# Eight storage orders for the split weights, and pairs for four chunks of x, in a two-layer fp32 decoder trunk

## The chip, the cores and the metric

One core of one Trainium2 chip runs the whole program in one launch. The metric is device microseconds of that core, the median of three runs.

## The reference

Two layers; each normalises x (512 tokens, 2048 features), makes one wide projection, runs two attention groups of eight heads on it, gates them, projects back and adds. Everything is fp32.

```python
for l in range(DEPTH):                       # 2
    h = _rms_norm(x, norm_g[l])
    proj = jnp.einsum('bsd,de->bse', h, w_in[l])
    q_a, k_a, v_a, z_a, c_q, c_kv, k_r, z_b = jnp.split(proj, split_points, axis=-1)
    ...
    o_a = _diff_attention(qa, ka, va, lam, rel_bias_table)     # 8 heads, two softmax maps each
    ...
    q_b = jnp.einsum('bsr,re->bse', _rms_norm(c_q, mla_q_norm_g[l]), w_uq[l])
    kv = jnp.einsum('bsr,re->bse', _rms_norm(c_kv, mla_kv_norm_g[l]), w_ukv[l])
    ...
    o_b = _mla_attention(q_nope, q_rope, k_nope, k_rope, v_b)  # 8 heads
    ...
    mixed = jnp.concatenate([o_a, o_b], axis=-1)
    x = x + jnp.einsum('bse,ed->bsd', mixed, w_out[l])
return _rms_norm(x, final_norm_g)
```

## The kernel before

x is kept feature-major: sixteen chunks of 128 features by 512 tokens. An fp32 product is made of three passes in the rounded type fp32r: each operand is split into a high part (the rounded copy) and a low part (what rounding left), and `mm3` adds high by high, high by low and low by high into one PSUM bank. A matmul has a stationary operand, 128 by 128, which a weight load (PEld in the profile) brings into the array, and a moving operand, mostly 128 by 512, which streams past it. In `mm3` the weight part is stationary and the x part moves. In `job_v` it is the other way round.

The weights come as 290 blocks of 128 by 1024, in the order in which TensorE uses them. `WStream` fetches block i into a buffer `raw` (two of them, two blocks ahead), and one block ahead of its use splits it: ScalarE casts `raw` into `whi` (L94), VectorE subtracts into `wlo` (L95). Each of `whi` and `wlo` has two buffers, so the split of the next block waits until TensorE is done with the one before the current one. A full block of `mm3` work is 8 chunks by 3 passes, 24 matmuls.

A block has a kind. "std" is the usual one; "kr" is one block per layer with its own layout; a callable kind puts a few blocks into a slot of another tile. The blocks of `b_kouter` (the first projection of layer 0, chunk by chunk as x arrives, and the diff group's V) and of `b_uv` (the MLA group's V) are "std" too.

`split_into` splits the chunks of x into tiles `x0` to `x15`, one tile per chunk, which holds the high part in its first 512 words and the low part in the next 512. The same tiles `x0` to `x7` are reused at the end of a layer for the gated outputs of the MLA heads, which are the first half of the operands of the output projection (`job_out_half`).

The order of the work on TensorE and of the DMA issues on SyncE and GpSimd is written out by hand (`run_jobs` walks the jobs and slips attention steps between them). The order on ScalarE and VectorE is left to the framework's scheduler.

Of the kernel before, what the change touches and what calls it, by code (L numbers as in the profile page):

```python
# [9 lines left out]
F32 = mybir.dt.float32  # L10
F32R = mybir.dt.float32r
AF = mybir.ActivationFunctionType
ALU = mybir.AluOpType
AX = mybir.AxisListType

P = 128
T = 512
# [44 lines left out]
class WStream:  # L62
# [3 lines left out]
    def __init__(self, nc, pool, src, dma_ahead=2, split_ahead=1):  # L66
        self.nc, self.pool, self.src = nc, pool, src
        self.descs, self.raw, self.parts = [], {}, {}
        self.nd = self.ns = self.i = 0
        self.da, self.sa = dma_ahead, split_ahead  # L70
# [7 lines left out]
    def _split(self, i):  # L78
        nc = self.nc
        _, width, kind = self.descs[i]  # L80
        r = self.raw.pop(i)
        if callable(kind):
            a, b = kind()
        else:
            a = self.pool.tile([P, 1024], F32R, tag="whi", name=f"whi{i}", bufs=2)
            b = self.pool.tile([P, 1024], F32R, tag="wlo", name=f"wlo{i}", bufs=2)
        if kind == "kr":
            for t, k0 in ((a, 0), (b, 8)):
                tv = t.rearrange("p (k s c) -> p k s c", s=2, c=64)
                rv = r.rearrange("p (k c) -> p k c", c=64)[:, k0:k0 + 8, :]  # L90
                nc.scalar.copy(out=tv[:, :, 0, :], in_=rv)
                nc.vector.tensor_tensor(out=tv[:, :, 1, :], in0=rv, in1=tv[:, :, 0, :].bitcast(F32), op=ALU.subtract)
        else:
            nc.scalar.copy(out=a[:, :width], in_=r[:, :width])  # L94
            nc.vector.tensor_tensor(out=b[:, :width], in0=r[:, :width], in1=a[:, :width].bitcast(F32), op=ALU.subtract)  # L95
        self.parts[i] = (a, b)
# [12 lines left out]
    def get(self, ahead=True):  # L109
        i = self.i  # L110
        self.i += 1
        if ahead:
            self.ahead()
        return self.parts.pop(i)


def fold(w):

    return w.reshape(-1, P, w.shape[1]).transpose(1, 0, 2).reshape(P, -1)
# [25 lines left out]
def trunk(ctx, tc, blocks, xf, gains, diff_lambda, rel_bias_table, onehot, tables, wb, outf):  # L145
    nc = tc.nc
# [8 lines left out]
    def t_(shape, dt, tag, bufs):  # L155
        uid[0] += 1
        return sb.tile(shape, dt, tag=tag, name=f"{tag}_{uid[0]}", bufs=bufs)
# [8 lines left out]
    def f32(ap):  # L166
        return ap.bitcast(F32)
# [6 lines left out]
        return (lambda a: fold(a[w[0]][w[1]][r0:r0 + 1024, c0:c0 + P])), 1024, kind  # L174

    def b_kouter(w, c0, j):
        return (lambda a: fold(a[w[0]][w[1]][j * 256:(j + 1) * 256, c0:c0 + T])), 1024, "std"

    def b_kr(w):
        return (lambda a: fold(a[w[0]][w[1]][:, C_KR:C_KR + 64])), 1024, "kr"  # L180
# [15 lines left out]
    def b_uv(l, q, j):  # L196

        def block(a):
            w = a["w_ukv"][l][j * 256:(j + 1) * 256, q * 1024:(q + 1) * 1024]
            return fold(w.reshape(256, 4, 256)[:, :, P:].reshape(256, T))  # L200
        return block, 1024, "std"


    ident = sb.tile([P, P], F32, name="ident")
# [51 lines left out]
    def split_into(k, src, scale):  # L256

        both = t_([P, 2, T], F32R, f"x{k}", 1)
        hi, lo = both[:, 0, :], both[:, 1, :]
        if scale is None:  # L260
            nc.scalar.copy(out=hi, in_=src)
            nc.vector.tensor_tensor(out=lo, in0=src, in1=f32(hi), op=ALU.subtract)
        else:
            nc.scalar.activation(out=hi, in_=src, func=AF.Copy, scale=scale)
            nc.vector.scalar_tensor_tensor(out=lo, in0=src, scalar=scale, in1=f32(hi), op0=ALU.mult, op1=ALU.subtract)
        return hi, lo

    def load_x(k):
        if k % 2 == 0 and XA + k < KC:
            fetch_x(XA + k, 2, nc.sync)  # L270
        xh[k], xl[k] = split_into(k, xt[k], g_norm(0, k))
        square_into(xt[k], k, KC - 1)
# [68 lines left out]
    def job_kouter(src2d, c0, accs, xload):  # L341
        ws.descs += [b_kouter(src2d, c0, j) for j in range(8)]

        def gen():
            accs.extend([p_("s", 2), p_("s", 2), p_("o", 1), p_("acc", 3)])
            ws.ahead()
            xload(0)
            for j in range(8):
                hi, lo = ws.get()
                if j == 0:  # L350
                    xload(1)
                for kk in range(2):
                    kc = 2 * j + kk
                    if kc + 2 < KC:
                        xload(kc + 2)
                    for i in range(4):
                        c = slice(kk * T + i * P, kk * T + (i + 1) * P)
                        mm3(accs[i], hi[:, c], lo[:, c], xh[kc], xl[kc], kc == 0, kc == KC - 1)
                    yield
        return 16, gen  # L360
# [511 lines left out]
    xnew, pairs = {}, {}  # L872
    for l in range(DEPTH):
# [33 lines left out]
        def v_mla(q, l=l, ckvn=ckvn):  # L907
            return job_v([b_uv(l, q, j) for j in range(2)], lambda kc: (ckvn[kc][:, 0, :], ckvn[kc][:, 1, :]), None)

        def v_diff(q, wi=wi):  # L910
            return job_v([b_kouter(wi, C_V + q * T, j) for j in range(8)], lambda kc: (xh[kc], xl[kc]), True)
# [13 lines left out]
        def split_mix(i, mix=mix, ms=mslot):  # L925
            def f():
                ms[i] = split_into(i, mix[8 + i], None)
            return f

        def out_evac(d, l=l):  # L930
            def f(acc):
                r = st["res"].pop(d)
                xn = t_([P, T], F32, "ma", 8) if d < 8 else tmp()
                nc.vector.tensor_tensor(out=xn, in0=acc, in1=r, op=ALU.add)
                nc.gpsimd.dma_start(out=xres[l + 1][d], in_=xn)
                square_into(xn, d, KC - 1)
                if d >= 8:
                    xh[d], xl[d] = split_into(d, xn, g_norm(l + 1, d))
                xnew[d] = xn
            return f  # L940
# [151 lines left out]
```

## Time and profile before

| | |
|---|---|
| median of 3 runs | 1840.79 us (1840.78 to 1840.84) |
| the profiled execution | 1841.41 us, its span 1839.6 us |
| TensorE matmul (PE) busy | 1795.7 us, 98% |
| weight loads (PEld) busy | 1488.3 us, beside the matmuls |
| VectorE (DVE) busy | 1021.9 us, 56% |
| ScalarE (ACT) busy | 878.8 us, 48% |
| TensorE clock granted, mean | 0.99 of full |

A matmul's listed duration is longer than the distance to the next one, because matmuls are pipelined. What one of them costs is read from the starts of two that follow each other; the text calls this distance the pitch.

### The profile page before, as it was taken

What the parts mean: (1) busy time and instruction counts of PE and PEld (TensorE: products, weight loads), DVE (VectorE), ACT (ScalarE), POOL (GpSimd) and SP (SyncE); (2) the same over time, 40 slices, a digit from 0 to 9 for tenths busy, and PEclk for the clock granted to TensorE, in tenths of its full rate; (3) what the DMA queues carried; (4) which work ended last, traced back from release to release, by engine and by line L of the source; (5) the groups of instructions that cost most, each with busy time, mean ns of one, the idle gap of its engine ahead of it and who ended that gap; (6) DMA issues with size and microseconds to landing.
All of it is one profiled execution on the core that took longest, in us unless ns stands there. A gap on an engine that the chain in (4) does not pass through costs nothing.

```text
span 1839.6 us, 21822 instructions
## 1 busy us (share of the span) xinstructions
PE 1795.7 (98%) x8348; PEld 1488.3 (81%) x8348; DVE 1021.9 (56%) x1903; ACT 878.8 (48%) x1548; POOL 38.0 (2%) x74
## 2 busy tenths in 40 slices
PE   9958999999999999999999999999999999999997
PEld 7837888888888888888888888888888888888886
DVE  6616556553777366743355565465366654784334
ACT  6406555542666355622344466465355544663332
POOL 0000000000000000010000000000000000000000
PEclk9978999999999999999999999999999999999999
DMA  5352222223222332344432322222332323233333
GB/s 212 95 85 80 73 71 89 83 86 96 93 83 78 103 92 86 97 138 147 145 121 92 96 75 65 75 91 85 95 91 87 94 90 92 77 92 119 119 116 131
DMA packets 55621, 181.11 MB, mean 98 GB/s; under 512 B 6908, under 2 KB 11004, under 8 KB 55517
## 3 DMA queue, kind: packets, MB, share of 16 engines
q1 hardware_dynamic: 48828, 159.00, 27.7%
q0 software_dynamic: 6400, 20.19, 4.5%
q8 instruction: 66, 1.08, 0.2%
q10 hardware_dynamic: 288, 0.52, 0.1%
q14 instruction: 39, 0.31, 0.1%
HBM read 168.68 MB, written 11.01 MB: 98 GB/s over the span
## 4 chain that ended last, share of the span: by engine, by line
PE 94%; DMA 3%; DVE 2%; ACT 1%; issue 0%; DVEq 0%; ACTq 0%; SPq 0%
PE pacc L319 23%; PE pacc L321 23%; PE pacc L320 23%; PE pacc L428 3%; PE pacc L430 3%; PE pacc L429 3%; DMA raw<-in_blocks_dram 3%; PE ptp L672 2%; PE po L689 1%; PE po L690 1%; PE po L688 1%; PE po L428 1%; PE ps L320 1%; PE po L430 1%; PE po L429 1%; PE ps L321 1%
## 5 line engine op out<-in xcount | busy, mean ns | idle before, releaser
L94 ACT CAST whi<-raw 128x1024 fp32r<-128x1024 f32 (+1 forms) x282 | 292.2, 1037 | 634.9 <-PE pacc L320 428.1
L319 PE MATMUL pacc<-x,whi 128*128 128x512 f32 (+1 forms) x1472 | 583.1, 396 | 11.5 <-ACT whi L94 11.5
L321 PE MATMUL pacc<-x,wlo 128*128 128x512 f32 (+1 forms) x1472 | 575.1, 391 | 0.0
L320 PE MATMUL pacc<-x,whi 128*128 128x512 f32 (+1 forms) x1472 | 574.4, 390 | 0.0
L95 DVE TENSOR_TENSOR wlo<-raw,whi 128x1024 fp32r<-128x1024 f32 (+1 forms) x282 | 340.8, 1208 | 340.9 <-ACT whi L94 332.3
L319 PEld LDWEIGHTS pacc<-x,whi 128*128 128x128 f32 x1472 | 278.2, 189 | 63.7 <-ACT whi L94 12.0
L321 PEld LDWEIGHTS pacc<-x,wlo 128*128 128x128 f32 x1472 | 277.2, 188 | 60.0 <-DVE wlo L95 0.8
L320 PEld LDWEIGHTS pacc<-x,whi 128*128 128x128 f32 x1472 | 277.8, 189 | 50.9
L319 PE MATMUL pacc<-mb,whi 128*128 128x512 f32 (+1 forms) x400 | 158.5, 396 | 0.0
L321 PE MATMUL pacc<-mb,wlo 128*128 128x512 f32 (+1 forms) x400 | 156.4, 391 | 0.7 <-DVE wlo L95 0.7
L320 PE MATMUL pacc<-mb,whi 128*128 128x512 f32 (+1 forms) x400 | 156.3, 391 | 0.0
L665 ACT ACTIVATE sa<-sa,m 128x128 f32<-128x128 f32 (+3 forms) x128 | 71.9, 561 | 119.2 <-DVE m L663 118.2
L663 DVE CUSTOM_DVE_ANT_0 sa<-ps,cs 128x128 f32<-128x128 f32 (+3 forms) x128 | 62.2, 486 | 83.3 <-PE ptp L672 30.7
L539 DVE TENSOR_TENSOR tmp<-pacc,rstd 128x512 f32<-128x512 f32 x64 | 44.1, 689 | 94.9 <-PE pacc L321 94.9
L321 PEld LDWEIGHTS pacc<-mb,wlo 128*128 128x128 f32 x400 | 75.2, 188 | 19.1 <-DVE wlo L95 1.5
L320 PEld LDWEIGHTS pacc<-mb,whi 128*128 128x128 f32 x400 | 75.3, 188 | 16.3
L319 PEld LDWEIGHTS pacc<-mb,whi 128*128 128x128 f32 x400 | 75.3, 188 | 16.1
L678 ACT CAST pth<-ptp 128x128 fp32r<-128x128 f32 (+3 forms) x128 | 53.7, 420 | 46.8 <-PE ptp L672 46.5
L428 PE MATMUL pacc<-whi,x 128*128 128x512 f32 x192 | 75.9, 395 | 0.0
L430 PE MATMUL pacc<-whi,x 128*128 128x512 f32 x192 | 74.8, 390 | 0.0
L429 PE MATMUL pacc<-wlo,x 128*128 128x512 f32 x192 | 74.8, 390 | 0.0
L679 DVE TENSOR_TENSOR ptl<-ptp,pth 128x128 fp32r<-128x128 f32 (+3 forms) x128 | 61.7, 485 | 4.2 <-ACT pth L678 2.4
(247 smaller groups left out, 2347.6 us busy)
## 6 DMA issues: line engine op xcount, KB each, us to landing
raw<-in_blocks_dram SPq DMA_DIRECT2D x282, 512.0 KB, 3.5
cs<-brow POOLq DMA_DIRECT2D x16, 256.0 KB, 3.0
cs<-in_x_dram POOLq DMA_DIRECT2D x16, 256.0 KB, 4.2
cs<-xres POOLq DMA_DIRECT2D x16, 256.0 KB, 2.9
out_dram<-x SPq DMA_DIRECT2D x16, 256.0 KB, 2.2
mb<-in_x_dram SPq DMA_DIRECT2D x7, 512.0 KB, 6.5
brow<-pth POOLq DMA_DIRECT2D x1, 2560.0 KB, 56.6
raw<-in_blocks_dram SPq DMA_DIRECT2D x8, 256.0 KB, 2.6
```

The costliest lines, as they stand in the source:

```text
L94: nc.scalar.copy(out=a[:, :width], in_=r[:, :width])
L95: nc.vector.tensor_tensor(out=b[:, :width], in0=r[:, :width], in1=a[:, :width].bitcast(F32), op=ALU.subtract)
L319: nc.tensor.matmul(acc, wh, rh, start=first, stop=False)
L320: nc.tensor.matmul(acc, wh, rl, start=False, stop=False)
L321: nc.tensor.matmul(acc, wl, rh, start=False, stop=last)
L428: nc.tensor.matmul(accs[t], xhi[:, c], hi[:, w], start=kc == 0, stop=False)
L429: nc.tensor.matmul(accs[t], xhi[:, c], lo[:, w], start=False, stop=False)
L430: nc.tensor.matmul(accs[t], xlo[:, c], hi[:, w], start=False, stop=kc == n - 1)
L663: nc.vector.tensor_tensor_reduce(out=s[:, :n], in0=ps[:, :n], in1=bias, scale=-scale, scalar=3.0e38, op0=ALU.add, op1=ALU.min, accum_out=m ...
L665: nc.scalar.activation(out=s[:, :n], in_=s[:, :n], func=AF.Exp, scale=-1.0, bias=m[:, 0:1], accum_out=m[:, 1:2])
L678: nc.scalar.copy(out=view(h["ph"]), in_=pv)
L679: nc.vector.tensor_tensor(out=view(h["pl"]), in0=pv, in1=f32(view(h["ph"])), op=ALU.subtract)
```

## The change

A std block gets one tile `w` of 2048 + 48 words in place of `whi` and `wlo`. Where the words of the high and the low part lie in it goes by the block's number modulo eight: "apart" is the order of before (each part is one run of 1024 words); in "pairs" the high and the low word of one weight lie side by side, so that a part is read and written in steps of 2 words (8 bytes), at four different starts (0, 16, 32 and 48 words into the tile); in "groups" the eight chunks lie innermost, so that one chunk's 128 words lie 8 words (32 bytes) apart; in "both" they lie 16 words (64 bytes) apart; the eighth is "apart" 16 words further on. The blocks of `b_kouter` and `b_uv` become "plain": two runs of 1024 as before, in the common tile. Four chunks of x, 4 to 7, have their two parts in pairs (steps of 8 bytes), in the input projections as in the output projection.

```diff
-            a = self.pool.tile([P, 1024], F32R, tag="whi", name=f"whi{i}", bufs=2)
-            b = self.pool.tile([P, 1024], F32R, tag="wlo", name=f"wlo{i}", bufs=2)
+            t = self.pool.tile([P, 2048 + 48], F32R, tag="w", name=f"w{i}", bufs=2)
+            a, b = t[:, :1024], t[:, 1024:2048]
+            if kind == "std":
+                va, vb = laid(t, i % len(WAYS))
+                n = width // P
+                rv = r.rearrange("p (g m) -> p g m", m=P)[:, :n, :]
+                nc.scalar.copy(out=va[:, :n, :], in_=rv)
+                nc.vector.tensor_tensor(out=vb[:, :n, :], in0=rv, in1=va[:, :n, :].bitcast(F32), op=ALU.subtract)
+                self.parts[i] = tuple(Laid(lambda g, v=v: v[:, g, :]) for v in (va, vb))
+                return
...
+def laid(t, way):
+
+    kind, off = WAYS[way]
+    t = t[:, off:off + 2048]
+    if kind == "apart":
+        v = [t[:, i * 1024:(i + 1) * 1024].rearrange("p (g m) -> p g m", m=P) for i in range(2)]
+    elif kind == "pairs":
+        v = [t.rearrange("p (g m s) -> p g m s", m=P, s=2)[:, :, :, i] for i in range(2)]
+    elif kind == "groups":
+        v = [t[:, i * 1024:(i + 1) * 1024].rearrange("p (m g) -> p g m", m=P) for i in range(2)]
+    else:
+        v = [t.rearrange("p (m g s) -> p g m s", m=P, s=2)[:, :, :, i] for i in range(2)]
+    return v
...
+WAYS = (("apart", 0), ("pairs", 0), ("pairs", 16), ("pairs", 32), ("pairs", 48), ("groups", 0), ("both", 0), ("apart", 16))
...
     def b_kouter(w, c0, j):
-        return (lambda a: fold(a[w[0]][w[1]][j * 256:(j + 1) * 256, c0:c0 + T])), 1024, "std"
+        return (lambda a: fold(a[w[0]][w[1]][j * 256:(j + 1) * 256, c0:c0 + T])), 1024, "plain"
...
         both = t_([P, 2, T], F32R, f"x{k}", 1)
+        if 4 <= k < 8:
+            both = both.rearrange("p a b -> p (a b)").rearrange("p (t s) -> p s t", s=2)
         hi, lo = both[:, 0, :], both[:, 1, :]
```

The order of TensorE's 8121 rows, of SyncE's and of GpSimd's is the same in both programs. On ScalarE and VectorE, whose order the scheduler makes, splits move by a few places against their neighbours. The first place shown is ScalarE early in layer 0, around the splits of blocks 12 and 13 (`whi_690` and `whi_730` before, `w_678` and `w_717` now; `kr` is the shared rotary key, `mb` the normalised query compression). Before:

```order
L284 ACTIVATE tmp_648<-tmp_649 128x512
L94 CAST whi_690<-raw_621 128x1024
L592 CAST kr_579<-tmp_574 64x512
L593 CAST kr_578<-tmp_574 64x512
L285 ACTIVATE tmp_648<-tmp_648 128x512
L295 ACTIVATE gate_685<-ma_683 128x512
L286 ACTIVATE tmp_650<-tmp_648 128x512
L94 CAST whi_730<-raw_688 128x1024
L543 CAST mb_659<-tmp_657 128x512
```

The same place now:

```order
L326 ACTIVATE tmp_636<-tmp_637 128x512
L634 CAST kr_569<-tmp_564 64x512
L635 CAST kr_568<-tmp_564 64x512
L327 ACTIVATE tmp_636<-tmp_636 128x512
L337 ACTIVATE gate_673<-ma_671 128x512
L328 ACTIVATE tmp_638<-tmp_636 128x512
L91 CAST w_678<-raw_610 128x1024
L91 CAST w_717<-raw_676 128x8x128
L585 CAST mb_647<-tmp_645 128x512
```

The cast of block 12 has moved behind five small operations, and the cast of block 13 ("groups", written as 8 runs of 128) follows it at once.

The second place is VectorE shortly after, where the bias rows (`pth`) are copied out of PSUM; their DMA to DRAM is issued behind the second copy. Before:

```order
L95 TENSOR_TENSOR wlo_731<-raw_688,whi_730 128x1024
L544 TENSOR_TENSOR mb_674<-tmp_672,mb_674 128x512
L817 TENSOR_REDUCE es<-tmp_706 128x4
L832 COPY pth_748<-ptp_749 8x512
L832 COPY pth_748<-ptp_752 8x128
L539 TENSOR_TENSOR ma_768<-pacc_687,rstd_504 128x512
```

The same place now:

```order
L857 TENSOR_TENSOR tmp_693<-v_574 128x128 x2
L874 COPY pth_734<-ptp_735 8x512
L586 TENSOR_TENSOR mb_662<-tmp_660,mb_662 128x512
L859 TENSOR_REDUCE es<-tmp_693 128x4
L874 COPY pth_734<-ptp_738 8x128
L581 TENSOR_TENSOR ma_754<-pacc_675,rstd_494 128x512
```

The first copy now stands ahead of two operations that it stood behind; the second is still the last of the four, so the DMA's place is the same to within one short operation.

## Rows read from the trace of the kernel before

**Rows 1.** The page, part 1: engine, busy us, share of the span, instructions.

```profile
PE 1795.7 (98%) x8348; PEld 1488.3 (81%) x8348; DVE 1021.9 (56%) x1903; ACT 878.8 (48%) x1548; POOL 38.0 (2%) x74
```

**Rows 2.** Busy time by stretch, with the granted clock (PEclk).

```profile
core 0: us, PE busy (x) PEld busy (x) DVE busy (x) ACT busy (x) POOL busy (x), PEclk, DMA share, GB/s
92.00:138.00 46.00, 23.14 (x89) 17.43 (x88) 5.57 (x6) 3.26 (x4) 0.00 (x0) 0.79 0.56 85
...
460.00:800.00 340.00, 340.00 (x1586) 282.63 (x1585) 221.26 (x459) 188.93 (x354) 6.45 (x12) 1.00 0.31 94
```

**Rows 3.** Timeline of TensorE near 1000 and 1185 us: start, duration, instruction.

```profile
1000.03 0.39 PE L319 MATMUL pacc<-x,whi 128*128 128x512 f32 x1
...
1005.47 0.39 PE L319 MATMUL pacc<-x,whi 128*128 128x512 f32 x1
...
1182.60 0.34 PE L688 MATMUL po<-pth,v 128*128 128x384 f32 x1
1182.78 0.34 PE L689 MATMUL po<-ptl,v 128*128 128x384 f32 x1
...
1183.13 0.39 PE L319 MATMUL pacc<-x,whi 128*128 128x512 f32 x1
1183.36 0.40 PE L320 MATMUL pacc<-x,whi 128*128 128x512 f32 x1
...
1184.51 0.28 PE L688 MATMUL po<-pth,v 128*128 128x256 f32 x1
1184.63 0.28 PE L689 MATMUL po<-ptl,v 128*128 128x256 f32 x1
...
1186.32 0.27 PE L320 MATMUL ps<-ka,qa 128*128 128x128 f32 x1
1186.43 0.27 PE L321 MATMUL ps<-ka,qa 128*128 128x128 f32 x1
```

**Rows 4.** Busy time in one stretch at the low clock (columns as in Rows 2).

```profile
141.00:146.00 5.00, 3.06 (x7) 2.14 (x8) 2.62 (x5) 3.63 (x6) 0.00 (x0) 0.50 0.42 108
```

**Rows 5.** Timeline of TensorE in that stretch.

```profile
144.26 0.63 PE L319 MATMUL pacc<-mb,whi 128*128 128x512 f32 x1
144.69 0.63 PE L320 MATMUL pacc<-mb,whi 128*128 128x512 f32 x1
145.12 0.63 PE L321 MATMUL pacc<-mb,wlo 128*128 128x512 f32 x1
```

**Rows 6.** Groups by line and shape: busy us, mean ns, idle before and its releasers.

```profile
L319 PE MATMUL pacc<-x,whi 128*128 128x512 f32 x1456 | 578.6, 397 | 11.5 <-ACT whi L94 11.5
L95 DVE TENSOR_TENSOR wlo<-raw,whi 128x1024 fp32r<-128x1024 f32 x274 | 335.3, 1224 | 335.1 <-ACT whi L94 330.4 <-PE pacc L371 3.8 <-issue 0.3
L94 ACT CAST whi<-raw 128x1024 fp32r<-128x1024 f32 x274 | 287.4, 1049 | 632.2 <-PE pacc L320 425.4 <-PE pacc L430 100.8 <-issue 51.1
```

**Rows 7.** The waits: who for whom, us in total, times, longest.

```profile
ACT whi L94 <- PE pacc L320: 428.1, 153, 8.6
DVE wlo L95 <- ACT whi L94: 332.3, 173, 16.7
...
PE pacc L319 <- ACT whi L94: 11.5, 1, 11.5
```

**Rows 8.** The chain that ended last, one of two such pieces near 100 us.

```profile
89.14 23.86 DMA raw<-in_blocks_dram
```

**Rows 9.** DMA issues: KB each, median us to landing.

```profile
raw<-in_blocks_dram SPq DMA_DIRECT2D x282, 512.0 KB, 3.5
...
brow<-pth POOLq DMA_DIRECT2D x1, 2560.0 KB, 56.6
```

More of the change, by code (lines that the diff above doesn't have):

```diff
@@ L114, in get, with __init__, __getitem__ @@
         return self.parts.pop(i)
+class Laid:
+    def __init__(self, f):
+        self.f = f
+    def __getitem__(self, key):
+        c = key[1]
+        assert c.start % P == 0 and c.stop == c.start + P
+        return self.f(c.start // P)
+def laid(t, way):
[11 more added lines that the diff above has]
+WAYS = (("apart", 0), ("pairs", 0), ("pairs", 16), ("pairs", 32), ("pairs", 48), ("groups", 0), ("both", 0), ("apart", 16))
 def fold(w):
@@ L200, in block @@
             return fold(w.reshape(256, 4, 256)[:, :, P:].reshape(256, T))
-        return block, 1024, "std"
+        return block, 1024, "plain"
     ident = sb.tile([P, P], F32, name="ident")
```

## The prediction, made before the changed kernel ran

> **What bounds the kernel now.** I read the page's busy times first. TensorE's matmuls fill 98% of the span, the other engines about half [rows 1]. The waits say the same: TensorE stood still for a late cast once, for 11.5 us [rows 7]. What it loses lies mostly in one place, and that wait belongs to it: from 92 to 138 us it is busy for 23 of 46 us [rows 2], while two weight blocks take 23.9 us each to arrive [rows 8] beside the 2.5 MB DMA of the bias rows, which takes 56.6 us [rows 9]. So the time is the sum of the matmuls' pitches plus about 44 us (1839.6 - 1795.7), and an edit counts if it changes a pitch or makes a split late.
>
> The timeline gives the pitches. At full clock a 512-column matmul follows the one before after 0.23 us (1183.13, 1183.36), more exactly 0.227 us (24 of them from 1000.03 to 1005.47), and 384 columns after 0.175, 256 after 0.12, 128 after 0.11 [rows 3]. Each has its own weight load. From 512 to 256 columns the pitch falls in step with the columns (256 columns, 0.107 us, at 2.4 GHz). At 128 it stops falling, so 0.11 us is what a load of 128 by 128 needs, and under a 512-column matmul it has some 0.117 us to spare. Where the granted clock is at its lower level, 1.2 GHz [rows 4], the 512-column pitch is 0.427 us [rows 5], the columns alone.
>
> **The change part by part.**
>
> *TensorE, moving side.* No instruction is added or moved on TensorE. What changes is how operands are read. Chunks 4 to 7 of x are now read in steps of 8 bytes. The count: 76 input-projection jobs of 16 chunks and 30 output columns of 8 give the 1456 matmuls of the row for L319 [rows 6] (76 x 16 + 30 x 8). Of these 76 x 4 + 30 x 4 = 424 use chunks 4 to 7, times three passes 1272; the first projection adds 4 x 4 x 3 = 48 and the two rotary-key jobs 16. That is 1336 matmuls of 512 columns, and the last two output columns, done in halves, add 48 of 256.
>
> No row shows a matmul with a stepped moving operand, so the price has two ends. The lower one is nothing. The upper one is the nearest row in which the stream itself runs at half rate, 0.427 us: +0.200 us each. I take the upper end. The reason is a comparison of readers. The moving stream reads 512 words of 4 bytes in 0.213 us, 9.6 bytes per ns and partition; the ScalarE cast reads 1024 words in 1.049 us, 3.9 bytes per ns [rows 6]. TensorE's stream is by far the fastest reader in the trace, and with both parts side by side it has to step over 4096 bytes to get its 2048. If the storage can hand out no more than the run of bytes which it hands out now, the stream takes twice as long; for a slower reader the same step would be free. Sum: 1336 x 0.200 = 267.2 us, and 48 x (0.427 / 2 - 0.12) = 4.5 us, together 271.7 us.
>
> A rule speaks against this term. The Trainium skill, page "SBUF — State Buffer", section "Door 1: The DMA port swizzle", says that SBUF has 16-byte lines and that two hits on a line are enough for full bandwidth. By it a step of 8 bytes, two words to a line, would be free, and this term would be 0; only the steps of 32 and 64 bytes would cost. The page does not say for how fast a reader; no run here shows it yet, and I keep the comparison of rates.
>
> *TensorE, stationary side.* Of the std blocks 132 lie in pairs, 29 in groups and 25 in both. Their loads read 128 words in steps of 8, 32 or 64 bytes. One load may grow from 0.11 to 0.227 us before a 512-column matmul shows it, so double costs nothing (0.22). I take 0 for all three. The upper end for groups and both: a load three times as long, 0.327 us, would add 0.100 us to each of their matmuls. There are 29 x 24 - 12 (one block is half as long) + 25 x 24 = 1284, of which 264 have a slowed moving stream on top that hides it: 1020 x 0.1 = 102 us.
>
> *ScalarE and VectorE.* The 186 stepped blocks are written in steps, and VectorE reads the high part in steps too. Now a split takes 1.049 + 1.224 us [rows 6], and ScalarE waits for TensorE to free the buffer 153 times, 428 us in all [rows 7]. From there until the block is wanted there is a block's work, 24 x 0.227 = 5.45 us. If both operations doubled, a split would take 4.55 us and still be in time, and VectorE's busy time would grow by 186 x 1.2 = 223 us, to 1245 of some 2110. In the fullest long stretch, 460 to 800 us, it is busy for 221 of 340 us [rows 2]. I take 0. The upper end, where groups and both take so long that each of 54 blocks comes 1 us late, is 54 us. The common tile adds a little: the cast waits for the last matmul of the freed block (L321) where it waited for the last that reads the high part (L320), 0.227 us earlier. The 3.2 us that the split has left cover it; behind the waiting cast stand softmax and gate operations, which TensorE meets some us later.
>
> *Order.* The scheduler moves splits by a few places on both engines; the bias rows' DMA keeps its place to within one operation of about 0.7 us, so its 44 us of loss stay, give or take 3.
>
> Sum against the profiled execution: 1841.4 + 271.7 = 2113.1 us. The median of the runs shown is 0.6 us below the profiled one: **2113 us**, and 2095 to 2135 if the mechanism is the right one (a pitch that keeps the 14 ns which a matmul now has above its columns would add 19 us).
>
> **The rivals.**
>
> *Loads too slow as well.* Steps of 32 and 64 bytes stretch a load beyond 0.227 us. Three times the present one gives 2113 + 102 = 2215 us; the late splits may come on top, to 2260. For it: nothing in the trace shows how a stepped load behaves. Against: it needs more than double.
>
> *Moving stream free, loads or splits not.* Then the 1284 loads show in full, up to 128 us, or the splits of 54 blocks are late: 1860 to 1970 us. This is what the 16-byte rule would give, priced by these rows.
>
> *Nothing shows.* All reads and writes are free or hidden: 1841 us. For it: three engines have slack of half the span, and the load half its pitch. Against: the moving stream has no slack at all.
>
> *Faster.* The 14 ns by which a 512-column pitch exceeds 512 columns at 2.4 GHz (0.227 against 0.213) could be a collision between the part that is loaded and the part that streams, which another layout ends. Some 7,000 matmuls would give back at most 97 us: 1744 us. It would decide if pitches of blocks in pairs fell below 0.227 us. Against: the excess is the same at 384 and at 256 columns (0.175 and 0.12 against 0.160 and 0.107), so it belongs to the matmul and not to its data.
>
> *Small loss.* Only a few late splits, 1845 to 1860 us.
>
> **How the numbers follow.** Chances: forecast 0.36, loads too 0.24, moving free but loads or splits not 0.16, nothing 0.14, small loss 0.06, faster 0.04. The range from 1838 to 2230 us leaves out the faster case and the upper half of the second, 0.16 in all. A measurement of this kernel can tell 0.2% (3.7 us) from no change; by that, slower 0.82, same 0.14, faster 0.04.
>
> **What would show it.** In the profile after: 512-column matmuls on chunks 4 to 7 with a pitch near 0.43 us, in every block, whatever its order, while chunks 0 to 3 and 8 to 15 keep 0.227; blocks in groups and both with the same pitch as the others; TensorE still without waits for splits. It is wrong if chunks 4 to 7 keep 0.227 (then the first term falls), if blocks 5 and 6 of each eight show longer pitches (then the loads count), or if TensorE waits for `w`.

## The result and the profile after

The changed kernel takes 2178.81 us (median of four runs, 2178.11 to 2179.75) against 1840.78: 1.184 times the time before, 95% interval 1.182 to 1.186, so 338 us more. The forecast was slower, 2113 us in a range from 1838 to 2230. The direction and the main mechanism held. The time lies 66 us above the forecast, and above the 2095 to 2135 us which the prediction gave for its mechanism alone; where the 66 us lie is shown below.

Part 1 of the page of the changed kernel (columns as in [rows 1]):

```profile
PE 2133.9 (98%) x8348; PEld 1627.7 (75%) x8348; DVE 1075.0 (49%) x1903; ACT 940.6 (43%) x1548; POOL 37.9 (2%) x74
```

TensorE's matmuls are busy for 338 us longer and it stands idle for as long as before: 44.1 us (2178.0 - 2133.9) against 43.9. So the loss is all in the pitches of matmuls. VectorE and ScalarE work 53 and 62 us more, and the waits of TensorE show that this cost next to nothing (line, who it waited for, us in total, times, longest):

```profile
PE ptp L354 <- ACT sa L349: 15.7, 1, 15.7
PE pacc L361 <- ACT w L91: 7.5, 1, 7.5
...
PE pacc L363 <- DVE w L92: 0.5, 1, 0.5
```

L361 to L363 are the lines L319 to L321 of before, L91 and L92 the splits of a std block. The 15.7 us were 15.8 before. The 7.5 us are the place near the bias rows' DMA that cost 11.5 in [rows 7]. The groups by line and shape show where the time sits:

```profile
L361 PE MATMUL pacc<-x,w 128*128 128x512 f32 x1456 | 692.2, 475 | 7.5 <-ACT w L91 7.5
...
L92 DVE TENSOR_TENSOR w<-raw,w 128x1024 fp32r<-128x1024 f32 x226 | 326.7, 1446 | 422.5 <-ACT w L91 421.5
L91 ACT CAST w<-raw 128x1024 fp32r<-128x1024 f32 x226 | 303.0, 1341 | 731.8 <-PE pacc L363 568.1 <-issue 95.8 <-DMA raw<-in_blocks_dram 46.6
...
L361 PE MATMUL pacc<-mb,w 128*128 128x512 f32 x384 | 156.0, 406 | 0.0
```

The row for L361 with x answers to L319 in [rows 6]: a mean of 475 ns in place of 397, while the same line streaming from mb stands at 406. A mean mixes chunks, so the timeline is needed (start, duration, instruction):

```profile
1272.49 0.40 PE L362 MATMUL pacc<-x,w 128*128 128x512 f32 x1
1272.72 0.39 PE L363 MATMUL pacc<-x,w 128*128 128x512 f32 x1
...
1273.30 0.62 PE L361 MATMUL pacc<-x,w 128*128 128x512 f32 x1
1273.74 0.63 PE L362 MATMUL pacc<-x,w 128*128 128x512 f32 x1
1274.19 0.64 PE L363 MATMUL pacc<-x,w 128*128 128x512 f32 x1
```

Up to 1272.72 the chunks are contiguous and a matmul follows after 0.23 us; from 1273.30 on, on a chunk in pairs, after 0.45 us. TensorE runs the same 8348 matmuls in the same order before and after, so the time from each one's start to the next one's can be compared matmul by matmul. Sorted by what is streamed and by the order of the weights loaded beside it, with the median pitch of either kernel in us and the sum of the differences:

| streamed | weights loaded beside | matmuls | before | after | sum, us |
|---|---|---|---|---|---|
| x in pairs | any | 1384 | 0.227 | 0.453 to 0.459 | 301.3 |
| contiguous x | pairs | 1519 | 0.227 | 0.232 | 6.9 |
| contiguous x | groups | 379 | 0.227 | 0.246 | 8.4 |
| contiguous x | both | 317 | 0.227 | 0.238 | 4.8 |
| contiguous x | apart, 64 bytes off | 343 | 0.227 | 0.232 | 1.7 |
| contiguous x | apart, from the start | 548 | 0.227 | 0.231 to 0.233 | 2.4 |
| mb | pairs | 650 | 0.233 | 0.232 | 0.3 |
| mb | groups, both | 284 | 0.233 | 0.242, 0.237 | 2.2 |
| the rest (attention, v, norms, idle time) | | | | | 9.8 |

Together 337.8 us. (The 1384 are the 1336 of the prediction and 48 of 256 columns.) All tiles of x have moved by 384 bytes in this kernel, so the table by itself cannot part what the order of the weights costs from what the place of x costs; e2, e3 and e7 do that.

### The profile page after: what moved, and what is told of

It reads as the page before. It is cut to its first block, busy times and chain, and to the rows that moved or that the text cites. A ratio compares the mean times of both kernels' runs of the same rounds, so it can differ in the third digit from the quotient of the medians.

```text
span 2178.0 us, 21801 instructions
## 1 busy us (share of the span) xinstructions
PE 2133.9 (98%) x8348; PEld 1627.7 (75%) x8348; DVE 1075.0 (49%) x1903; ACT 940.6 (43%) x1548; POOL 37.9 (2%) x74
## 4 chain that ended last, share of the span: by engine, by line
PE 94%; DMA 2%; DVE 2%; ACT 1%; issue 0%; DVEq 0%; ACTq 0%; SPq 0%
PE pacc L361 24%; PE pacc L362 24%; PE pacc L363 24%; PE pacc L470 3%; PE pacc L471 3%; PE pacc L472 3%; DMA raw<-in_blocks_dram 2%; PE ptp L714 2%; PE ps L362 1%; PE ps L363 1%; PE po L732 1%; PE ps L361 1%; PE po L731 1%; PE po L470 1%; PE po L472 1%; PE po L471 1%
## 5 line engine op out<-in xcount | busy, mean ns | idle before, releaser
L361 PE MATMUL pacc<-x,w 128*128 128x512 f32 (+1 forms) x1472 | 697.7, 474 | 7.5 <-ACT w L91 7.5
L363 PE MATMUL pacc<-x,w 128*128 128x512 f32 (+1 forms) x1472 | 685.5, 466 | 0.0
L362 PE MATMUL pacc<-x,w 128*128 128x512 f32 (+1 forms) x1472 | 685.4, 466 | 0.0
L91 ACT CAST w<-raw 128x1024 fp32r<-128x1024 f32 (+1 forms) x234 | 308.8, 1320 | 748.6 <-PE pacc L363 584.9
L92 DVE TENSOR_TENSOR w<-raw,w 128x1024 fp32r<-128x1024 f32 (+1 forms) x234 | 332.8, 1422 | 422.5 <-ACT w L91 421.5
L363 PEld LDWEIGHTS pacc<-x,w 128*128 128x128 f32 x1472 | 332.6, 226 | 123.8 <-issue 84.0
L361 PEld LDWEIGHTS pacc<-x,w 128*128 128x128 f32 x1472 | 331.4, 225 | 110.5 <-issue 68.5
L362 PEld LDWEIGHTS pacc<-x,w 128*128 128x128 f32 x1472 | 332.6, 226 | 101.3 <-issue 68.1
L361 PE MATMUL pacc<-mb,w 128*128 128x512 f32 (+1 forms) x400 | 160.7, 402 | 0.0
L363 PE MATMUL pacc<-mb,w 128*128 128x512 f32 (+1 forms) x400 | 157.3, 393 | 0.5 <-DVE w L92 0.5
L362 PE MATMUL pacc<-mb,w 128*128 128x512 f32 (+1 forms) x400 | 157.4, 394 | 0.0
L103 DVE TENSOR_TENSOR w<-raw,w 128x1024 fp32r<-128x1024 f32 x48 | 58.8, 1225 | 102.9 <-ACT w L102 102.7
L102 ACT CAST w<-raw 128x1024 fp32r<-128x1024 f32 x48 | 50.3, 1048 | 122.3 <-PE pacc L472 83.9
L361 PEld LDWEIGHTS pacc<-mb,w 128*128 128x128 f32 x400 | 88.9, 222 | 15.7 <-issue 4.9
L362 PEld LDWEIGHTS pacc<-mb,w 128*128 128x128 f32 x400 | 89.2, 223 | 15.4 <-issue 4.8
L363 PEld LDWEIGHTS pacc<-mb,w 128*128 128x128 f32 x400 | 88.7, 222 | 12.7 <-DVE w L92 0.9
L470 PE MATMUL pacc<-w,x 128*128 128x512 f32 x192 | 76.7, 400 | 0.0
L471 PE MATMUL pacc<-w,x 128*128 128x512 f32 x192 | 75.7, 394 | 0.0
L472 PE MATMUL pacc<-w,x 128*128 128x512 f32 x192 | 75.7, 394 | 0.0
```

The lines of the kernel that those rows point to most:

```text
L91: nc.scalar.copy(out=va[:, :n, :], in_=rv)
L92: nc.vector.tensor_tensor(out=vb[:, :n, :], in0=rv, in1=va[:, :n, :].bitcast(F32), op=ALU.subtract)
L361: nc.tensor.matmul(acc, wh, rh, start=first, stop=False)
L362: nc.tensor.matmul(acc, wh, rl, start=False, stop=False)
L363: nc.tensor.matmul(acc, wl, rh, start=False, stop=last)
L470: nc.tensor.matmul(accs[t], xhi[:, c], hi[:, w], start=kc == 0, stop=False)
```

## The experiments

Theory 1, the prediction's: the moving stream reads chunks 4 to 7 at half rate, and that is nearly all. Its rivals: the loads with a step show too, and something else slows all matmuls by 5 ns. Two further questions ran beside this one: what about a step halves the rate (e4, e5), and what the place of a tile costs (e2, e6, e7, e9).

**e1, pairs of x alone.** The kernel before with the change's two lines for x:

```
+        if 4 <= k < 8:
+            both = both.rearrange("p a b -> p (a b)").rearrange("p (t s) -> p s t", s=2)
```

> The kernel before, with chunks 4 to 7 of x in pairs and nothing else. Theory (the stepped moving stream is the cost, 0.453 us a pitch as the changed kernel shows it, against 0.227): 1336 x 0.226 + 48 x 0.11 = 307 us more, some us less for the stall near 100 us, so 2140 to 2150 us. Rival (my forecast's price, 0.427 us): 2113 us. Rival (the stepped stream is slow only beside stepped weights): under 2100 us.

Measured: 2140.13 us, ratio 1.1627 (1.1608 to 1.1647), 300 us more. The median pitch of the 512-column matmuls on these chunks is 0.452 us, that of the others 0.227 as before.

```profile
L321 PE MATMUL pacc<-x,whi 128*128 128x512 f32 x1456 | 677.7, 465 | 5.4 <-ACT whi L94 5.4
```

```profile
1253.53 0.63 PE L321 MATMUL pacc<-x,whi 128*128 128x512 f32 x1
1253.98 0.63 PE L322 MATMUL pacc<-x,whi 128*128 128x512 f32 x1
1254.43 0.63 PE L323 MATMUL pacc<-x,wlo 128*128 128x512 f32 x1
...
1255.50 0.40 PE L321 MATMUL pacc<-x,whi 128*128 128x512 f32 x1
1255.73 0.39 PE L322 MATMUL pacc<-x,whi 128*128 128x512 f32 x1
```

So the term stands by itself: 1336 x 0.225 and 48 x 0.107 (256 columns, 0.120 to 0.227) are 306 us, less 6.5 us that TensorE stands idle less (mostly the 5.4 in the row above where [rows 7] have 11.5).

**e2, the shift alone.** The change's weight tiles are 48 words longer each, so that all tiles behind them lie 384 bytes further on. Here that is all that is done:

```
+        if k == 0 and "pad" not in st:
+            st["pad"] = sb.tile([P, 96], F32, name="pad")
         both = t_([P, 2, T], F32R, f"x{k}", 1)
```

> The kernel before, with an unused tile of 96 words (384 bytes) ahead of x0, which moves the x tiles from a multiple of 2048 bytes to 384 bytes above one, as the 48 spare words of each of the two w buffers do in the changed kernel. Theory (where a moving operand starts sets 5 ns of its pitch): pitches of unstepped matmuls rise from 0.227 to about 0.232 us, 1855 to 1863 us. Rival (those 5 ns in the changed kernel come from its stepped neighbours): 1841 us.

Measured: 1862.8 us, ratio 1.0121 (1.0106 to 1.0136). In the timeline 24 matmuls on contiguous x take from 442.48 to 448.08, 0.233 us each, where the kernel before has 0.227 [rows 3]:

```profile
442.48 0.40 PE L321 MATMUL pacc<-x,whi 128*128 128x512 f32 x1
...
448.08 0.40 PE L321 MATMUL pacc<-x,whi 128*128 128x512 f32 x1
```

Nothing about these matmuls differs but the place from which they stream.

**e3, the orders of the weights alone.** The changed kernel without the two lines of e1, and with 256 spare words in place of 48, so that x is contiguous and at multiples of 2048 bytes:

```
-            t = self.pool.tile([P, 2048 + 48], F32R, tag="w", name=f"w{i}", bufs=2)
+            t = self.pool.tile([P, 2048 + 256], F32R, tag="w", name=f"w{i}", bufs=2)
...
-        if 4 <= k < 8:
-            both = both.rearrange("p a b -> p (a b)").rearrange("p (t s) -> p s t", s=2)
```

> The changed kernel with x unstepped, and 256 spare words in a w buffer in place of 48, so that the x tiles start at multiples of 2048 bytes again. Theory (loads in steps of 32 and 64 bytes last 0.249 and 0.221 us and set the pitch): 684 x 0.018 + 600 x 0.010 = 18 us more, 1855 to 1862 us, blocks in pairs at 0.227. Rival (my forecast, all loads and splits hidden): 1841 us. Rival (late splits beside it): over 1870 us, with waits of TensorE for w.

Measured: 1884.76 us, ratio 1.0239 (1.0224 to 1.0254): 44 us more, over twice what was expected. The time is that of the last rival, but its waits did not come: TensorE waited for a late split 1.0 us, and 1.2 us longer at the place near the bias rows. Compared matmul by matmul with before, groups and both make 21 us, with pitches of 0.245 (24 matmuls from 841.87 to 847.75) and 0.236 us, as expected. But beside loads in pairs the pitch of contiguous x is 0.233, and so it is beside parts apart that start 64 bytes off, 10 us together. That was not expected where x lies well.

```profile
841.87 0.41 PE L359 MATMUL pacc<-x,w 128*128 128x512 f32 x1
842.12 0.40 PE L360 MATMUL pacc<-x,w 128*128 128x512 f32 x1
...
847.75 0.39 PE L359 MATMUL pacc<-mb,w 128*128 128x512 f32 x1
```

Of the rest, 8 us are idle time: these two waits, and several of 0.2 to 1.1 us for operands of the norms and of attention.

**e10, all standard blocks in pairs.** It takes the surprise of e3 by itself: x as in e3, one order for all blocks.

```
-                va, vb = laid(t, i % len(WAYS))
+                va, vb = laid(t, 1)
```

> The changed kernel with x contiguous and at multiples of 2048 bytes, and all standard weight blocks in pairs from the start of their tile (a step of 8 bytes between the 128 words of a load, and between the words that ScalarE and VectorE write). Theory 'a load in pairs hides but for the 4 to 7 ns that any weights cost whose start lies off a multiple of 512 bytes or that have a step': 226 blocks x 24 x 0.005 = 27 us, and 2 us of lateness from ScalarE's 0.073 us per split: 1869 us (1863 to 1878). Rival 'a load in pairs costs nothing, as its duration of 0.195 us against 0.188 says': 1841 us within 3. Second rival 'pairs cost as much as the steps of 32 and 64 bytes': 18 ns, 1939 us and more.

Measured: 1862.52 us, ratio 1.0118 (1.0101 to 1.0135), 22 us more (just under the 1863 of the theory) and the pitch 0.233 in all of these blocks, beside loads of the high part, which starts at a multiple of 512 bytes, as beside those of the low part. So a load in pairs is not free, though its own duration hardly shows it: 0.195 us against 0.188 before.

```profile
L360 PEld LDWEIGHTS pacc<-x,w 128*128 128x128 f32 x1472 | 286.2, 194 | 49.8
...
L92 DVE TENSOR_TENSOR w<-raw,w 128x1024 fp32r<-128x1024 f32 x226 | 276.8, 1225 | 271.0 <-ACT w L91 269.6
L91 ACT CAST w<-raw 128x1024 fp32r<-128x1024 f32 x226 | 254.7, 1127 | 544.2 <-PE pacc L361 404.2 <-issue 72.4 <-DMA raw<-in_blocks_dram 46.9
```

VectorE does its 1024 elements in pairs in 1225 ns, as it does contiguous ones (1224 in [rows 6]); ScalarE's cast grows from 1049 to 1127.

**e8, all standard blocks in groups.** The same with `laid(t, 5)`: every load and every split has a step of 32 bytes.

> The changed kernel with x contiguous and at multiples of 2048 bytes, and all standard weight blocks in the one order with the chunks innermost (a step of 32 bytes between the 128 words of a load, and of 32 bytes between the words that ScalarE and VectorE write) in place of one block in eight. Theory 'a load with a step of 32 bytes still hides beside a matmul but for some 18 ns, and the splits (2.2 + 2.2 us) stay ahead of TensorE's 24 matmuls per block': 226 blocks x 24 x 0.018 = 98 us, and 10 to 30 us of lateness of ScalarE and VectorE behind 265 and 225 us more of work: 1950 to 1970 us, the pitch 245. Rival 'the splits become the bound once every block has a long one': PE waits for the split by L91 or L92 in most blocks, over 60 us of waits, 2000 to 2100 us. Second rival 'the loads add up beside each other': the pitch 0.30 or more, over 2200 us.

Measured: 2013.48 us, ratio 1.0939 (1.0924 to 1.0954), 173 us more, above the 1950 to 1970 of the theory and within the range of the first rival, whose waits did not come:

```profile
L360 PEld LDWEIGHTS pacc<-x,w 128*128 128x128 f32 x1472 | 485.3, 330 | 2.3 <-DVE x L305 0.7
...
L92 DVE TENSOR_TENSOR w<-raw,w 128x1024 fp32r<-128x1024 f32 x226 | 514.6, 2277 | 364.6 <-ACT w L91 364.5
L91 ACT CAST w<-raw 128x1024 fp32r<-128x1024 f32 x226 | 502.3, 2223 | 453.5 <-PE pacc L361 350.6 <-DMA raw<-in_blocks_dram 46.6 <-issue 35.3
```

```profile
PE pacc L359 <- ACT w L91: 13.3, 1, 13.3
PE pacc L361 <- DVE w L92: 10.2, 12, 2.2
PE ps L795 <- DVE ka L691: 6.5, 16, 1.1
```

Casts and subtractions take twice as long, and TensorE waits for a split by VectorE 12 times, 10 us in all: the splits stay nearly ahead even when all of them are long. Idle time grows by 33 us (2012.3 - 1935.5 against 43.9), a third of it in waits for late splits and the rest in small waits for operands of attention and the norms. The median pitch is 0.245. Compared matmul by matmul, the 512-column matmuls beside such a load take 114 us more, idle time left out; 35 of these lie in 259 matmuls that take 0.35 us or more to the next one, where the kernel before has 24. Most of the 259 (188) come directly behind a matmul of attention:

```profile
737.77 0.49 PE L712 MATMUL ptp<-ident,sb 128*128 128x128 f32 x3
738.01 0.61 PE L359 MATMUL pacc<-x,w 128*128 128x512 f32 x1
738.46 0.41 PE L360 MATMUL pacc<-x,w 128*128 128x512 f32 x1
```

The 270 in that place have a median of 0.409 us to the next where the kernel before has 0.283. A load of 0.33 us has less to hide under behind such short matmuls, but no run shows this by itself. The last 26 us lie in other matmuls and are not explained.

**e4, forms of runs, first set.** The kernel before, with chunks 4 to 7 laid out as runs (shown are words of the tile, offset, words spanned, step in runs, length of a run, tile):

```
+            words, off, n, s, w, name, i, j = ((1024, 0, 1024, 2, 2, "xa", 0, 1), (1536, 2, 1024, 2, 4, "xb", 0, 1),
+                (2048, 0, 2048, 4, 1, "xc", 0, 2), (None, 0, 2048, 4, 1, "xc", 1, 3))[k - 4]
...
+            v = t[:, off:off + n].rearrange("p (t s w) -> p s t w", s=s, w=w)
+            hi, lo = v[:, i], v[:, j]
```

> The kernel before, with four layouts for chunks 4 to 7: chunk 4 in runs of 2 words (two of the high part, two of the low part), chunk 5 in runs of 4 words that start 8 bytes past a multiple of 16, chunks 6 and 7 in one tile, each word 16 bytes from the next of its part. The V projection of the diff group, where x is stationary, reads chunks 0 and 1 in place of 4 and 5. Theory (the stream takes one 16-byte line in about 1.72 ns, whatever it uses of it): pitches 0.453 for chunks 4 and 5, about 0.89 for 6 and 7, 2440 us. Rival (it fetches pairs of neighbouring words, 8 bytes): 0.227 for 4 and 5, 0.453 for 6 and 7, 1992 us. Rival (any step that is not one word halves the rate): 0.453 for all four, 2143 us.

Measured: 2148.78 us in its one run, a span of 2147.0. The first theory (2440) fell; the time is near the 2143 of the last rival. All four chunks are slow, with pitches of 0.451 (xa, runs of two), 0.451 to 0.467 (xb, runs of four from 8 bytes behind a 16-byte multiple) and 0.461 us (xc, one word in four).

```profile
L344 PE MATMUL pacc<-xc,whi 128*128 128x512 f32 x210 | 135.1, 644 | 0.0
...
L345 PE MATMUL pacc<-xb,whi 128*128 128x512 f32 x105 | 67.1, 639 | 0.0
...
L345 PE MATMUL pacc<-xa,whi 128*128 128x512 f32 x105 | 66.3, 631 | 0.0
```

xc spans twice the bytes of a chunk in pairs and costs 2% more. So the price does not go by the bytes stepped over, and runs of two or of misplaced four bring nothing back. Two readings were left: any step halves the rate, or only whole, aligned lines of four words escape.

**e5, forms of runs, second set.** The same with other numbers:

```
+            words, off, n, s, w, name, i, j = ((1024, 0, 1024, 2, 4, "xa", 0, 1), (1536, 1, 1024, 2, 2, "xb", 0, 1),
+                (1024, 0, 1024, 2, 1, "xc", 0, 1), (1024, 0, 1024, 2, 8, "xd", 0, 1))[k - 4]
```

> The kernel before, with x chunk 4 in runs of four words from a multiple of 16 bytes (tile xa: four words of the upper part, four of the lower), chunk 5 in runs of two words from one word behind such a multiple (xb), chunk 6 in pairs (xc, the control), chunk 7 in runs of eight words (xd). All V projections of the differential group read chunks 0, 1 and 3 in place of 4, 5 and 7, so the output isn't the reference's. Theory 'a step costs one word per cycle, and only whole aligned lines of 16 bytes come at full rate': the 512-column pitch is 0.227 to 0.232 us for xa and xd and 0.453 for xb and xc; two chunks of about 319 matmuls with 0.226 us more each and some 6 us for loads, 1841 + 144 + 6 = 1991 us (1984 to 2000). Rival 'whatever is not one contiguous run of words is read at half rate': 0.453 for all four and, by the kernel with four other forms of runs, 2140 us (2125 to 2150). Third: the rate depends on the length of a run alone, so that runs of two cost less than pairs and runs of four or eight nearly nothing: xb between 0.23 and 0.45, and 1920 to 1960 us.

Measured: 1992.75 us, ratio 1.0826 (1.0806 to 1.0846); the first theory said 1991, its rival 2140.

```profile
L345 PE MATMUL pacc<-xb,whi 128*128 128x512 f32 x105 | 66.8, 636 | 0.0
...
L345 PE MATMUL pacc<-xc,whi 128*128 128x512 f32 x105 | 66.6, 635 | 0.0
...
L345 PE MATMUL pacc<-xa,whi 128*128 128x512 f32 x105 | 41.6, 396 | 0.0
...
L345 PE MATMUL pacc<-xd,whi 128*128 128x512 f32 x105 | 41.4, 394 | 0.0
```

Runs of four (xa) and eight words (xd) from a multiple of 16 bytes are as fast as contiguous chunks (391 ns in the row of the same line for the other chunks), with median pitches of 0.229 to 0.235 us for the passes of xa and 0.231 to 0.233 for the second and third of xd (its first, right behind the chunk in pairs, has 0.255; the first pass behind the pairs has 0.248 in e1); pairs (xc) and runs of two off such a multiple (xb) stay at 0.44 to 0.46. xa steps over as many bytes as the pairs do.

**e7, the change with x in its old place.** The changed kernel with the 256 spare words of e3 and nothing else.

> The changed kernel with 256 spare words behind each pair of weight tiles in place of 48, so that x starts at multiples of 2048 bytes again; nothing else differs. Theory 'of the 338 us, about 22 come only from the 384 bytes by which the spare words push x': the matmuls with contiguous x beside a load of ways 0 and (in part) of the others come down from 232 by up to 5 ns, those with stepped x stay at 453. By the sum of the two parts measured apart, 1840.8 + 299.3 (pairs of x alone) + 43.9 (orders of the weights alone, x at multiples of 2048) = 2184 us at most; with stepped matmuls hiding their loads (1336 of some 7000, a fifth of the 44) 2175. Theory of a plain sum with the shift taken away: 2178.8 - 22.4 = 2156. Rival: the spare words matter nothing once the weights themselves lie off such multiples: 2178.8 within 2.

Measured: 2174.28 us, ratio 1.1812 (1.1796 to 1.1828): 4.5 us less than the changed kernel, near the 2175 of the sum in which stepped matmuls hide their loads. The plain sum, 2156, fell: the shift costs 22 us in a kernel whose weights lie well and 4.5 us here, because beside most of these weights the pitch is 0.233 either way. With e1 this parts the 338 us by runs alone: 300 us for x in pairs (e1), 34 us for the orders of the weights on top of that (2174.28 - 2140.13), and 4.5 us for the place of x.

**e6, mb at multiples of 2048 bytes.** In the kernel before the eight mb tiles start 64 bytes short of one. Two spare tiles move them there and leave the weights and x at such multiples:

```
+    sb.tile([P, 16], F32, name="pad")
...
+    sb.tile([P, 496], F32, name="pad2")
```

> The kernel before with 16 spare words ahead of the eight mb tiles and 496 behind them, so that these tiles (the normalised compressed q and kv, the mixed heads) start at a multiple of 2048 bytes in place of 64 bytes short of one; x, whi and wlo stay at multiples of 2048. Theory 'a 512-column matmul takes 227 ns where the moving words and the weights loaded beside it both start at a multiple of some 512 bytes, 4 to 6 ns more elsewhere': about 1131 matmuls that stream from mb beside a load from whi or wlo and 176 that stream from whi or wlo beside a load from mb come from 232 to 233 ns to 227, 1307 x 0.0055 = 7 us, 1834 us (1832 to 1836), ratio 0.9961. Rival 'not the start in memory but something else in these matmuls (their accumulators, the length of a group) sets the 233': no change, 1840.8 us within 1.

Measured: 1834.48 us, ratio 0.9967 (0.9955 to 0.9979), which beats both kernels. A half-job of 24 matmuls on mb took 0.2333 us each before (from 807.84 us); here it takes 0.2265 (23 steps from 804.85 to 810.06). Before:

```profile
807.84 0.39 PE L319 MATMUL pacc<-mb,whi 128*128 128x512 f32 x1
...
813.44 0.39 PE L319 MATMUL pacc<-x,whi 128*128 128x512 f32 x1
```

With mb moved:

```profile
804.85 0.39 PE L320 MATMUL pacc<-mb,whi 128*128 128x512 f32 x1
...
810.06 0.39 PE L322 MATMUL pacc<-mb,wlo 128*128 128x512 f32 x1
```

**e9, seven starts of x.** Spare words ahead of x1 to x7 and in x15:

```
+        if 1 <= k < 8 and ("pad", k) not in st:
+            st["pad", k] = sb.tile([P, (8, 8, 16, 32, 64, 128, 256)[k - 1]], F32, name=f"pad{k}")
+        if k == 15:
+            both = t_([P, 1024 + 8], F32R, "x15", 1)[:, 4:1028].rearrange("p (s t) -> p s t", s=2)
...
```

> The kernel before with spare words ahead of the tiles x1 to x7 and four in tile x15, so that the chunks of x start at other places: x1 32 bytes behind a multiple of 2048, x2 64, x3 128, x4 256, x5 512, x6 1024, x15 16 bytes; x0, x7 to x14, whi and wlo stay at multiples of 2048. Nothing else differs. Theory 'what costs the 5 ns is a start that is no multiple of 512 bytes': medians of the 512-column pitch beside a load from whi or wlo of 231 to 234 ns for x1, x2, x3, x4 and x15, and 227 for the others; 5 chunks x some 318 matmuls x 0.005 = 8 us, 1848.5 us. Rival 'the unit is 256 bytes': x4 at 227 too, 1847 us. Rival 'the unit is 2048 bytes, the length of a part': x5 and x6 at 232 too, 1852 us. Rival 'the 22 us of the shifted tiles came from something else than the start of the moving words (the other tiles behind x were shifted as well)': all chunks at 227, 1840.5 us.

Measured: 1847.63 us, ratio 1.0038 (1.0023 to 1.0053), 7 us more. Median pitches of the three passes in us, by chunk:

| chunk | start behind a multiple of 2048 bytes | pitch |
|---|---|---|
| x15 | 16 | 0.228 to 0.233 |
| x1, x2, x3 | 32, 64, 128 | 0.229 to 0.237 |
| x4 | 256 | 0.233 to 0.235 |
| x5, x6 | 512, 1024 | 0.227 to 0.233 |
| x0 | 0, unmoved, runs between x15 and x1 | 0.231 to 0.234 |
| x7 to x14 | 0 | 0.227, at most 0.230 |

That the start matters is confirmed. The times expected for a unit of 512 bytes (1848.5) and of 256 (1847) lie too close together to choose by, and in this table the chunks stand in each other's way: a chunk serves three matmuls in a row, and a pitch that was disturbed takes longer than that to come back. The kernel before shows this where nothing starts badly. Right behind a stretch with a pitch of 0.427 us, the nine matmuls from 13.02 on take 0.231 us each, up to 15.10 us; only then comes 0.227 (and the first three behind matmuls of attention have medians of 0.236, 0.233 and 0.231):

```profile
12.71 0.47 PE L321 MATMUL pacc<-x,wlo 128*128 128x512 f32 x1
13.02 0.39 PE L319 MATMUL ps<-x,whi 128*128 128x512 f32 x1
...
15.10 0.39 PE L319 MATMUL pacc<-x,whi 128*128 128x512 f32 x1
```

So x0, which was not moved and runs between x15 and x1, says nothing of its own place, nor do x4 to x6 behind x3. The first projection does, where each chunk serves twelve matmuls in a row. In e9 x3 starts there at 18.11 us, x4 at 20.89 and x5 at 23.61:

```profile
18.11 0.39 PE L324 MATMUL ps<-x,whi 128*128 128x512 f32 x1
...
20.89 0.39 PE L324 MATMUL ps<-x,whi 128*128 128x512 f32 x1
...
23.61 0.39 PE L324 MATMUL ps<-x,whi 128*128 128x512 f32 x1
```

x3, at 128 bytes, takes 0.232 us per matmul throughout; x4, at 256, takes 0.227, and so do x5 and x6. In this kernel a start at a multiple of 256 bytes costs nothing, and one at 16, 32, 64 or 128 bytes costs 3 to 7 ns. The theory of 512 bytes fell.

## Why the prediction was right, and where it was off

**The bound** held. Time is the sum of TensorE's pitches, and with 338 us of matmuls added no other engine came to bound it. That the time lies in the stated range is in part luck: the range reached up to 2230 for a rival in which loads alone cost 100 us, and what filled it was three smaller errors: 28 us in the price of the stream, 34 in the orders of the weights, 4.5 in the place of x.

**The moving side** was the right mechanism, and its size was off. The prediction took the upper row, 0.427 us [rows 5], +0.200 each, 271.7 us. Measured by e1 it is 0.452, +0.225 each, 300 us. The 14 ns that a pitch has above its columns (0.227 against 0.213) nearly double along with the columns; the text had seen 19 us of this as an upper edge, and should not have taken the low-clock row as a stand-in, since there the excess is gone (0.427 for 512 columns).

**The reason for it fell in part.** That the fastest reader pays first fits the runs: VectorE reads and writes pairs in 1225 ns as before, ScalarE writes them 7% slower, the moving stream takes twice as long. That the price follows from the bytes it has to step over did not: e4's one word in four costs 0.461, not twice 0.453, and e5's runs of four step over just as much for nothing. Of the forms tried in the two runs, a 512-column stream of 4-byte words keeps its full rate in those that take whole 16-byte pieces from a 16-byte multiple (runs of four and of eight), and runs at half rate in every other (steps of 8 and 16 bytes, runs of two, runs of four 8 bytes off). What in the storage makes it so is not shown.

The Trainium skill, page "SBUF — State Buffer", section "Door 1: The DMA port swizzle", says that two hits on a 16-byte line are enough for full bandwidth, and the prediction gave that the smaller chance. For the moving stream this case contradicts it (two words per line, 0.452 us against 0.227 in e1). For VectorE the runs agree with it: a step of 8 bytes costs nothing (1225 ns against 1224), and one of 32 bytes nearly doubles a subtraction (2277 in e8).

**The loads** were costed at nothing, with 102 us as the upper end. By the table above they cost 24 us: 7.2 beside pairs, 9.5 beside groups, 5.9 beside both and 1.7 beside parts apart that start 64 bytes off; with 6 us on stepped streams and 5 on other matmuls, idle time included, it is the 34 us between e1 and e7. The step that failed is "double costs nothing": loads of 0.195 to 0.33 us all show a little, from 5 to 19 ns per matmul, and a load that is only 4% longer (e10) shows 6. By the prediction's own sign (blocks 5 and 6 of each eight show longer pitches) this term was wrong. That a stepped stream hides them held but for 6 ns beside groups (0.453 to 0.459 us). The prediction also miscounted: 124 std blocks lie in pairs and not 132, 178 are stepped and not 186; VectorE's upper figure would be 214 us and not 223, and the forecast does not move. The rival "loads too slow as well" asked for 100 ns each and did not happen.

**The missed term** is the place: chunks 0 to 3 and 8 to 15 did not keep 0.227. The text looked at what each operand's step is and never at where the tiles start. The 48 spare words push x 384 bytes on, which alone costs 22 us (e2) and in the whole change 4.5 us (e7). In the table it is the 2.4 us of contiguous x beside well-placed weights and a part of the last row's 9.8, small amounts in attention, the norms and idle time.

**The splits and the order** held. Splits in groups and both take twice as long, and TensorE waits for one outside the place of [rows 7] for 0.5 us; its idle time is 44 us as before. e8 says how far the cover reaches: with all blocks in groups the late splits by VectorE cost TensorE 10 us.

**Faster** had argued with a collision between load and stream that a layout could end. The 14 ns stayed in every run; what a layout can win is the 6 ns of e6, and only where a tile starts badly.

## What to carry to other kernels

When parts of an operand are interleaved, interleave them in runs of four or eight 4-byte words (the two lengths tried) that start at a multiple of 16 bytes if TensorE streams them: single words or pairs of words halve its rate (0.227 to 0.453 us per 512 columns), which on 1336 of the matmuls cost 300 us, while VectorE does not notice pairs at all. A slower load is not simply free under a matmul that lasts longer than it: look at the pitch, not at the load's duration. Where thousands of matmuls set the time, look at the start addresses of the tiles they read: 64 spare bytes ahead of one group of tiles (and a filler behind it) gave 0.3%, 384 spare bytes ahead of another cost 1.2%, and in e9 multiples of 256 bytes were free.

## What the runs showed of the hardware that was not expected

- A 512-column fp32r matmul has a pitch of 0.227 us only where both the streamed words and the weights loaded meanwhile are contiguous and start well (at multiples of 256 bytes in e9); a bad start of either, or weights in pairs, costs 3 to 7 ns (0.230 to 0.234), and both together cost no more than one (mb, 64 bytes short, takes 0.233 before and 0.232 beside pairs).
- The stationary side bears a step far better than the moving side: steps of 8, 64 and 32 bytes cost 5, 10 and 18 ns per matmul. That 64 bytes cost less than 32 holds for the splits too: VectorE's by about 0.16 us, 2074 ns in the blocks in both against 2230 in those in groups of the changed kernel.
- A pitch that was disturbed comes back slowly: in the kernel before nine matmuls behind a slower stretch take 0.231 us each before it is 0.227 again, and in e9 the unmoved x0 loses 4 to 7 ns behind x15. A median over short stretches mixes this into the price of a layout; a long run of matmuls on one chunk does not. Why it lasts so long stays open.
